# Attention scores for two heads at a time in three PSUM banks, with the second passes over the keys on half of the rows for each head

## The chip, the cores and the metric

The kernel runs on one core of one Trainium2 chip. The metric is the device time of one execution in microseconds (us). Shown is the median of three runs; a further execution was taken with the hardware profiler.

## The reference

Two transformer-like blocks run one after the other on 512 tokens of width 1024, in f32. The first block normalizes and modulates the tokens, projects them, does windowed attention with a short convolution beside it, and then a mixture of 16 experts. The second block has a spatial gate, a convolution of 31 taps and a projection. The change lies in the attention of the first block:

```
def block(i):                        # one of 4 blocks of 128 queries
    qb = q[128 i : 128 i + 128]      # 16 heads of 64, 4 heads share one key head
    kb, vb = the keys and values of block i - 1, i, i + 1 (those that exist)
    s_lat = qb . kb / 8              # masked to a distance of at most 128
    s_ctx = qb . k_ctx / 8           # 256 context keys
    p = softmax(concat(s_lat, s_ctx, sink of the head))
    return p_lat . vb + p_ctx . v_ctx
```

The result has to agree with f32 arithmetic, so most matmuls are made of several passes in f32r: an operand x is split into a rounded part hi and a remainder lo, and products of the parts are summed.

## The kernel before, in words

**Stages.** The context manager `tile_two_blocks` writes out the program engine by engine in a fixed order (`manual_schedule`): each engine runs its instructions in the order of the code, and waits on semaphores for its operands and for buffers. First comes the modulation, the norm and the sums for keys and values (up to line 661, about 74 us). Then the attention stage follows (lines 663 to 947), which runs the query projections (`q_group`), the projections of the short convolution (`ct_chunk` with `conv_posts`) and the attention itself, interleaved. Behind it lie the merge, the router, the experts, whose weights stream from HBM, and the second block.

**PSUM.** PSUM has eight banks of 512 f32 a partition. The pool `psA` (line 97) has six single banks with the tag `b`, which all matmuls of the stage take in turn (`bank`, line 100), and one buffer of two banks, `bank2` (line 103), for scores; before the stage that buffer holds sums for keys and values (`kvc`).

**Queries and keys.** For a group of four heads that share a key head, `q_group` computes the queries, `rope` turns them, and `qst` (line 702) holds for each head 128 columns: 64 of hi (written by ScalarE, line 703) and 64 of lo (by VectorE, line 704, two steps later). `q_T` (line 684) transposes these by TensorE, so that `qTs[g]` holds for each head hi on partitions 0 to 63 and lo on 64 to 127. `kT[g]` (line 627) holds two matrices over 768 keys (512 tokens, 256 context): `z = 0` has the keys' hi on both halves of the partitions, `z = 1` their lo on both halves. A matmul of all 128 rows therefore gives (q_hi + q_lo) . k_hi or (q_hi + q_lo) . k_lo.

**One block.** `Block` (line 819) is one of 16 pieces: key head g, query block b. A block at an end of the sequence (b = 0 or 3) sees 256 latent keys, one in the middle 384, and each 256 context keys. `scores(i)` (line 837) does one head: two passes over the latent keys (L846), two over the context keys (L849), all with 128 rows, into the buffer of two banks; one VectorE instruction (L852) adds the mask, takes the maximum and writes P to SBUF; a small one (L855) scales the maximum; ScalarE takes the exponential (L856). `normalize` (L861 to L866) divides by the sum on VectorE. `turn` transposes 128 columns of P of four heads (L872, L874), `value` multiplies with V (L881), two heads on two halves of the array's columns (`tile_position=(0, 64*h)`).

**Order.** The loop at the end (line 926) goes over the blocks; for each it makes five rounds, and in each of the first four it emits the scores of one head. Twice in each round `F.share()` emits a share of the projection steps, each of three matmuls (L297, L298, L299). `normalize` follows the scores of the last head, and in the rounds 0, 2 and 4 the block before is turned and multiplied with V:

```
for i in range(5):
    if new and i < 4:
        new.scores(i)
    F.share()
    if new and i == 3:
        new.normalize()
    if not i and older:
        older.late()
    if old:
        old.values(i)
    F.share()
```

`F.defer` puts a piece of work off by some steps. The weights of the next projection are split by ScalarE (L258) and VectorE (L256) while the one before runs; their loads are issued by SyncE (L218) when a buffer is free. Far behind, L1872 is a matmul on 64 rows between matmuls on 128 rows.

Of the kernel before, what the change touches and what calls it, by code (L numbers as in the profile page):

```python
# [9 lines left out]
F32 = mybir.dt.float32  # L10
F32R = mybir.dt.float32r
BF16 = mybir.dt.bfloat16
AF = mybir.ActivationFunctionType
OP = mybir.AluOpType
PSUM = bass.MemoryType.PSUM
# [3 lines left out]
NT = T // 128  # L19
# [44 lines left out]
def tile_two_blocks(ctx: ExitStack, tc: tile.TileContext, a, out):  # L64
    nc = tc.nc
    ACT, DVE, PE, POOL, SP = nc.scalar, nc.vector, nc.tensor, nc.gpsimd, nc.sync
# [27 lines left out]
    pe_ = ExitStack()  # L94
    ep = pe_.enter_context(tc.tile_pool(name="ep", bufs=6))
    pa = ExitStack()
    psA = pa.enter_context(tc.tile_pool(name="psA", bufs=6, space=PSUM))
    cur = {"ps": psA}

    def bank(name="pb", shape=(512,), dt=F32):  # L100
        return cur["ps"].tile([128] + list(shape), dt, name=name, tag="b")
# [1 line left out]
    def bank2(name="s2"):  # L103
        return cur["ps"].tile([128, 1024], F32, name=name, tag="s2", bufs=1)
# [6 lines left out]
    def C(name):  # L111
        s = CL[name]
        return cst[:, s] if s.stop <= nc0 else cst2[:, s.start - nc0:s.stop - nc0]

    ident = C("ident")
# [16 lines left out]
    for gi, g in enumerate(groups):  # L132
        r = 0
# [238 lines left out]
    F = Filler()  # L372


    p_ = bank()
# [156 lines left out]
    m0 = mod_rows(mws[0], ep)  # L532
# [26 lines left out]
    m0 = mod_rows(mws[1], ep)  # L559
# [22 lines left out]
    m0 = mod_rows(mws[2], ep)  # L582
# [11 lines left out]
    m0 = mod_rows(mws[3], ep)  # L594
# [12 lines left out]
    sp = pa.enter_context(tc.tile_pool(name="spA", bufs=2, reuse_waits="tile"))  # L607

    def rope(ps, t0):

        r = sp.tile([128, 2, 4, 64], F32, name="rope", tag="rope", bufs=1)
        s = sp.tile([128, 2, 4, 64], F32, name="ropes", tag="ropes", bufs=1)
        pv = ps.rearrange("p t (h d) -> p t h d", d=64)
        cs = C("cos").rearrange("p (t d) -> p t d", d=64)[:, t0:t0 + 2, None, :].to_broadcast([128, 2, 4, 64])
        DVE.tensor_mul(r, pv, cs)
        sn = C("sin").rearrange("p (t h z f) -> p t h z f", h=2, z=2, f=16)
        p5 = ps.rearrange("p t (q h z f) -> p t q h z f", h=2, z=2, f=16)
        s5 = s.rearrange("p t q (h z f) -> p t q h z f", h=2, z=2, f=16)
        for j in range(2):
            for h in range(2):  # L620
                DVE.tensor_mul(s5[:, j, :, h], p5[:, j, :, h, ::-1, :],
                               sn[:, t0 + j, None, h].to_broadcast([128, 4, 2, 16]))
        DVE.tensor_add(r, r, s)
        return r


    kT = [kv.tile([128, 2, 768], F32R, name=f"kT{g}", tag=f"kT{g}") for g in range(4)]
# [12 lines left out]
    def k_T(part, kst):  # L640
        for g in range(4):
            p_ = bank("pT", (2, 2, 128), F32R)
            for j in range(2):
                for z in range(2):
                    PE.transpose(p_[:, z, j, :], kst[:, j, g, z].rearrange("p a d -> p (a d)"), identr)
            dst = kT[g][:, :, part * 256:part * 256 + 256].rearrange("p z (j q) -> p z j q", j=2)
            ACT.activation(dst, p_.bitcast(F32), AF.Copy)
# [15 lines left out]
    sink8 = cp.tile([128, 16], F32, name="sink8")  # L663
# [4 lines left out]
    qTs = {}  # L668
# [9 lines left out]
    def q_group(g):  # L678
        i, w = nextw()
        nxt = W.steps(i + 1)  # L680
        qT = big("qT", [4, 512], F32R)
        qTs[g] = qT

        def q_T(tp, qst):
            for hp in range(2):
                p_ = bank("pT", (2, 2, 128), F32R)
                for hh in range(2):
                    for j in range(2):
                        PE.transpose(p_[:, hh, j, :], qst[:, j, 2 * hp + hh].rearrange("p a d -> p (a d)"), identr)
                dst = qT[:, 2 * hp:2 * hp + 2, tp * 256:tp * 256 + 256].rearrange("p i (j q) -> p i j q", j=2)  # L690
                ACT.activation(dst, p_.bitcast(F32), AF.Copy)
            if tp:
                qdone[0] = g

        for tp in range(2):
            pq = bank("pq", (2, 256))
            for j in range(2):
                for s, _ in enumerate(gemm_tc(pq[:, j], w, 2 * tp + j, hx)):
                    ahead(nxt, 8 * tp + 4 * j + s)
                    yield  # L700
            qr = rope(pq, 2 * tp)
            qst = sp.tile([128, 2, 4, 2, 64], F32R, name="qst", tag="qst", bufs=1)
            ACT.activation(qst[:, :, :, 0, :], qr, AF.Copy)
            F.defer(2, lambda qst=qst, qr=qr: DVE.tensor_sub(qst[:, :, :, 1, :], qr, qst[:, :, :, 0, :].bitcast(F32)))
            F.defer(9, lambda tp=tp, qst=qst: q_T(tp, qst))

    def ct_chunk(xs, post, hooks=None):
# [111 lines left out]
    class Block:  # L819


        def __init__(self, g, b):
            self.g, self.b = g, b
            self.kb = kb = [t for t in (b - 1, b, b + 1) if 0 <= t < NT]
            self.nl = nl = len(kb) * 128
            self.n = n = nl + 256

            if b == NT - 1:
                self.lo, self.co, self.s0, self.mask = 256, 0, 0, C("mask")[:, 0:512]
                self.keys = [4, 5] + kb  # L830
            else:
                self.lo, self.co, self.s0 = 512 - nl, 512, 512 - nl
                self.mask = C("mask")[:, 896 - n:]
                self.keys = kb + [4, 5]
            self.P, self.pt, self.nk = [], {}, n // 128

        def scores(self, i):
            g, kb, nl, n, lo, co = self.g, self.kb, self.nl, self.n, self.lo, self.co
            if not i:
                self.m4 = sp.tile([128, 4], F32, name="m4", tag="m4")  # L840
                self.sm = sp.tile([128, 4], F32, name="sm", tag="sm")
            m4, sm = self.m4, self.sm
            s2 = bank2()
            q = qTs[g][:, i, self.b * 128:self.b * 128 + 128]
            for z in range(2):
                PE.matmul(s2[:, lo:lo + nl], q, kT[g][:, z, kb[0] * 128:kb[0] * 128 + nl], start=(z == 0),  # L846
                          stop=(z == 1))
            for z in range(2):
                PE.matmul(s2[:, co:co + 256], q, kT[g][:, z, 512:768], start=(z == 0), stop=(z == 1))  # L849
            p_ = sp.tile([128, 640], F32, name="P", tag="P", bufs=8)  # L850
            self.P.append(p_)
            DVE.tensor_tensor_reduce(p_[:, :n], s2[:, self.s0:self.s0 + n], self.mask, 1.0,  # L852
                                     sink8[:, 4 * g + i:4 * g + i + 1], op0=OP.add, op1=OP.max,
                                     accum_out=m4[:, i:i + 1])
            DVE.tensor_scalar(m4[:, i:i + 1], m4[:, i:i + 1], -0.125, None, op0=OP.mult)  # L855
            ACT.activation(p_[:, :n], p_[:, :n], AF.Exp, bias=m4[:, i:i + 1], scale=0.125, accum_out=sm[:, i:i + 1])  # L856

        def normalize(self):
            g, sm = self.g, self.sm
# [8 lines left out]
        def turn(self, kk):  # L868

            p_ = bank("pT", (4, 128))  # L870
            for i in range(4):
                PE.transpose(p_[:, i, :], self.P[i][:, kk * 128:kk * 128 + 128], ident)  # L872
            self.pt[kk] = sp.tile([128, 2, 2, 128], F32, name="PT", tag="PT", bufs=4)
            ACT.activation(self.pt[kk], p_.rearrange("p (i h) q -> p i h q", h=2), AF.Copy)  # L874

# [26 lines left out]
    def order():  # L902
        n = 0
        for g in range(4):
            if g < 3:
                yield q_group(g + 1)
            for post in conv_posts(g):
                hooks = {}
                if n < 8:
                    if n % 2 == 0:  # L910
                        macc = sp.tile([128, 512], F32, name="macc", tag="macc", bufs=1)
                    hooks = mod_hooks(n % 2, macc, False, lambda c=24 + 2 * (n - 1), m=macc: mod_columns(c, m))
                yield ct_chunk(hx, post, hooks)
                n += 1

    todo = list(order())
    F.defer(6, lambda: k_T(0, kst[0]))
    F.defer(13, lambda: k_T(1, kst[1]))
    F.defer(20, lambda: k_T(2, kst[2]))
# [6 lines left out]
    for n, new in enumerate(blocks):  # L926
        if new:
            while qdone[0] < new.g:
                F.fill(1)
        for i in range(5):  # L930
            if new and i < 4:
                new.scores(i)
            F.share()
            if new and i == 3:
                new.normalize()
# [5 lines that stand above are left out]
        older, old = old, new  # L941
# [331 lines left out]
    x_, y_, d = l0, l1, 32  # L1273
    while d:
# [3 lines left out]
        x_, y_, d = y_, x_, d // 2  # L1278
# [19 lines left out]
    for t in range(NT):  # L1298
        PE.matmul(cnt[:, :, 16:32], ones, ge[:, t, None, 0:16].to_broadcast([128, NT, 16]), start=False,
                  stop=(t == NT - 1))  # L1300
# [152 lines left out]
    for p in range(8):  # L1453
# [21 lines left out]
        for n in range(2):  # L1475
            p_ = bank("pg", (4, 128))
# [231 lines left out]
    cin, co = {}, {}  # L1708
# [302 lines left out]
```

## Time and profile before

| what | value |
|---|---|
| median of 3 runs | 1662.72 us (1662.14 to 1664.51) |
| the profiled execution | 1664.67 us |
| its span, from the first to the last instruction | 1662.9 us |
| TensorE busy | 1613.8 us, 97% of the span |
| VectorE busy | 923.6 us, 56% |
| ScalarE busy | 565.7 us, 34% |
| mean granted TensorE clock | 0.997 |
| read from HBM | 333.62 MB |

The engines are called PE (TensorE matmul), PEld (TensorE weight load, which overlaps PE), DVE (VectorE), ACT (ScalarE), POOL (GpSimd) and SP (SyncE). L846 is line 846 of the kernel. Matmuls are pipelined, and the end of one is modelled, so a row can be longer than the distance to the next start. f32 matmuls that are not of the type f32r show as two records each. In a timeline, "x8" merges eight instructions of one line, and "[0.53 <-DVE m L852]" means that the engine stood idle for 0.53 us just before, until that instruction of VectorE ended.

### The profile page before, as it was taken

How to read it: one execution, taken by the hardware profiler on the slowest of the kernel's cores; microseconds unless marked ns; L12 is line 12 of the kernel's file. 1: busy time of each engine (PE TensorE's matmuls, PEld its weight loads, DVE VectorE, ACT ScalarE, POOL GpSimd, SP SyncE). 2: the span in 40 equal slices, each digit the busy share in tenths (PEclk: the TensorE clock that was granted, in tenths of full speed). 3: DMA queues.
4: the chain of work that ended last, by engine and by line, in shares of the span. 5: the costliest groups of instructions: out<-in, count | busy, mean ns of one | idle time of the engine just before them, and what ended most of it. 6: DMA issues, size and time to landing. Idle time of an engine off the chain costs nothing.

```text
span 1662.9 us, 20664 instructions
## 1 busy us (share of the span) xinstructions
PE 1613.8 (97%) x8266; PEld 1143.4 (69%) x8266; DVE 923.6 (56%) x1761; ACT 565.7 (34%) x1069; POOL 60.6 (4%) x74
## 2 busy tenths in 40 slices
PE   8999999999999999999999888999999999999998
PEld 5987878777888884333333333368898888877886
DVE  4667677665554342222132212178989999855555
ACT  4454545455223232000000000063335542354234
POOL 2000000000000000000000000010100001000000
PEclk9999999999999999999999999999999999999999
DMA  9223232212654599999999999943322323422341
GB/s 366 68 77 102 88 96 76 98 51 76 207 197 129 223 365 357 419 427 426 427 426 427 426 427 426 416 147 94 94 85 77 101 78 100 113 92 100 102 152 51
DMA packets 139412, 341.26 MB, mean 205 GB/s; under 512 B 6735, under 2 KB 91508, under 8 KB 115636
## 3 DMA queue, kind: packets, MB, share of 16 engines
q1 hardware_dynamic: 135504, 328.50, 52.6%
q0 software_dynamic: 2864, 8.67, 1.4%
q10 hardware_dynamic: 948, 2.76, 0.4%
q8 instruction: 65, 1.06, 0.3%
q14 instruction: 31, 0.25, 0.0%
HBM read 333.62 MB, written 6.29 MB: 204 GB/s over the span
## 4 chain that ended last, share of the span: by engine, by line
PE 43%; DMA 13%; DVE 2%; issue 1%; ACT 1%; POOL 0%; POOLq 0%; ACTq 0%; SPq 0%; DVEq 0%
PE pb L297 9%; PE pb L298 9%; PE pb L299 9%; DMA ew<-w_exp_up 5%; DMA ew<-w_exp_gate 5%; PE py L1382 3%; DMA ew<-w_exp_down 2%; PE pu L1382 2%; DMA xe<-x_d,ix 1%; PE pv L297 1%; PE pv L299 1%; PE pv L298 1%; PE pa__6391 L1382 1%; PE pa__6149 L1382 1%; PE pa__5907 L1382 1%
## 5 line engine op out<-in xcount | busy, mean ns | idle before, releaser
L256 DVE TENSOR_TENSOR wl<-wr,wh 128x512 fp32r<-128x512 f32 x340 | 230.5, 698 | 120.7 <-ACT wh L258 120.7
L258 ACT ACTIVATE wh<-wr 128x512 fp32r<-128x512 f32 x340 | 195.2, 621 | 111.2 <-PE pb L298 58.3
L1722 DVE SCALAR_TENSOR_TENSOR co<-cin,cols,co 128x512 f32<-128x512 f32 x240 | 190.2, 793 | 4.2
L297 PE MATMUL pb<-h2h,wh 128*128 128x512 f32 x432 | 170.7, 395 | 0.0
L299 PE MATMUL pb<-h2h,wl 128*128 128x512 f32 x432 | 168.3, 390 | 0.0
L298 PE MATMUL pb<-h2l,wh 128*128 128x512 f32 x432 | 168.3, 390 | 0.0
L297 PE MATMUL pb<-hxh,wh 128*128 128x512 f32 x320 | 129.2, 404 | 0.0
L1382 PE MATMUL pu<-ew,xe 128*64 128x512 f32 x512 | 115.9, 595 | 10.0 <-DMA ew<-w_exp_up 10.0
L298 PE MATMUL pb<-hxl,wh 128*128 128x512 f32 x320 | 125.2, 391 | 0.0
L299 PE MATMUL pb<-hxh,wl 128*128 128x512 f32 x320 | 125.0, 391 | 0.0
L1382 PE MATMUL py<-ew,hb 128*64 128x512 f32 x440 | 102.4, 596 | 3.3 <-DMA ew<-w_exp_down 3.3
L297 PEld LDWEIGHTS pb<-h2h,wh 128*128 128x128 f32 x432 | 81.1, 188 | 19.0 <-issue 2.4
L1382 PEld LDWEIGHTS pu<-ew,xe 128*64 128x64 f32 x512 | 38.5, 137 | 80.3 <-issue 61.9
L299 PEld LDWEIGHTS pb<-h2h,wl 128*128 128x128 f32 x432 | 81.1, 188 | 17.1
L298 PEld LDWEIGHTS pb<-h2l,wh 128*128 128x128 f32 x432 | 81.1, 188 | 16.8 <-issue 0.5
L856 ACT ACTIVATE P<-P,m 128x512 f32<-128x512 f32 (+1 forms) x64 | 49.8, 778 | 98.6 <-DVE m L855 96.3
L1399 DVE TENSOR_TENSOR xr<-pg,xr 128x512 f32<-128x512 f32 x64 | 41.5, 686 | 69.4 <-PE pg L1398 68.1
L1473 DVE TENSOR_TENSOR hb<-pu,hb 128x512 f32<-128x512 f32 x16 | 10.3, 685 | 122.1 <-PE pu L1382 77.1
L1382 PEld LDWEIGHTS py<-ew,hb 128*64 128x64 f32 x440 | 32.7, 137 | 61.7 <-issue 52.8
L852 DVE CUSTOM_DVE_ANT_0 P<-s,cst,sink 128x512 f32<-128x512 f32 (+1 forms) x64 | 52.1, 814 | 38.2 <-PE s L849 37.8
L299 PEld LDWEIGHTS pb<-hxh,wl 128*128 128x128 f32 x320 | 60.1, 188 | 13.3
L297 PEld LDWEIGHTS pb<-hxh,wh 128*128 128x128 f32 x320 | 60.2, 188 | 10.9 <-issue 1.9
(479 smaller groups left out, 2990.6 us busy)
## 6 DMA issues: line engine op xcount, KB each, us to landing
ew<-w_exp_gate SPq DMA_DIRECT2D x64, 1024.0 KB, 19.4
ew<-w_exp_up SPq DMA_DIRECT2D x64, 1024.0 KB, 19.5
wr<-w_in SPq DMA_DIRECT2D x58, 1024.0 KB, 5.8
ew<-w_exp_down SPq DMA_DIRECT2D x55, 1024.0 KB, 20.7
wr<-w_mod SPq DMA_DIRECT2D x16, 1024.0 KB, 5.2
wm<-w_mod SPq DMA_DIRECT2D x8, 1024.0 KB, 12.0
wr<-w_out SPq DMA_DIRECT2D x8, 1024.0 KB, 5.1
ew<-w_exp_down SPq DMA_DIRECT2D x16, 512.0 KB, 10.5
```

What stands on the lines that cost most here:

```text
L256: (lo_engine or DVE).tensor_tensor(lo[:, ks], raw[:, ks], hi[:, ks].bitcast(F32), op=OP.subtract)
L258: ACT.activation(hi[:, ks], raw[:, ks], AF.Copy)
L297: PE.matmul(ps, ah, bh, start=first, stop=False)
L298: PE.matmul(ps, ah, bl, start=False, stop=False)
L299: PE.matmul(ps, al, bh, start=False, stop=last)
L852: DVE.tensor_tensor_reduce(p_[:, :n], s2[:, self.s0:self.s0 + n], self.mask, 1.0, sink8[:, 4 * g + i:4 * g + i + 1], op0=OP.add, op1=OP.ma ...
L856: ACT.activation(p_[:, :n], p_[:, :n], AF.Exp, bias=m4[:, i:i + 1], scale=0.125, accum_out=sm[:, i:i + 1])
L1382: PE.matmul(ps[64 * e:64 * e + 64, n], lhs(k, e), tiles[e][kk][:, n * 512:n * 512 + 512], start=(k == 0), stop=(k == KT - 1), tile_positio ...
L1399: DVE.tensor_add(xrow(t, half(n)), p_, xrow(t, half(n)))
L1473: DVE.tensor_mul(hb[:, 0, n * 512:n * 512 + 512], pu[:, n], hb[:, 0, n * 512:n * 512 + 512])
L1722: DVE.scalar_tensor_tensor(co[ct], cin[ct][:, k:k + 512], ctap(k, ct), co[ct], op0=OP.mult, op1=OP.add)
```

## The change

Three things are changed together. Scores are made for two heads at a time (`scores(u)`, u = 0 or 1, in the rounds 0 and 2) into a buffer `s3` of three banks; for that the PSUM pool is closed before the stage and a new one opened with five single banks beside it. For odd heads the parts of the query are swapped, so that hi lies on partitions 64 to 127. The second pass over a group of keys (z = 1) uses the hi part of the query alone, 64 rows, with `tile_position=(64*i, 0)`: even heads on the upper half of the array's rows, odd heads on the lower. That leaves out q_lo . k_lo there. Where the two heads' scores for a group lie in one bank (the context keys of a middle block), both passes keep 128 rows. The mask and the order of the columns follow the new places.

```
-    psA = pa.enter_context(tc.tile_pool(name="psA", bufs=6, space=PSUM))
-    cur = {"ps": psA}
+    pz = ExitStack()
+    cur = {"ps": pz.enter_context(tc.tile_pool(name="psA", bufs=6, space=PSUM, reuse_waits="tile"))}
...
             qst = sp.tile([128, 2, 4, 2, 64], F32R, name="qst", tag="qst", bufs=1)
-            ACT.activation(qst[:, :, :, 0, :], qr, AF.Copy)
-            F.defer(2, lambda qst=qst, qr=qr: DVE.tensor_sub(qst[:, :, :, 1, :], qr, qst[:, :, :, 0, :].bitcast(F32)))
+            q4 = qst.rearrange("p j (u i) a d -> p (j u) (i a) d", i=2)
+            q2 = qr.rearrange("p j (u i) d -> p (j u) i d", i=2)
+            ACT.activation(q4[:, :, 0::3], q2, AF.Copy)
+            F.defer(2, lambda q4=q4, q2=q2: DVE.tensor_sub(q4[:, :, 1:3], q2, q4[:, :, 0::3].bitcast(F32)))
...
+            self.full = len(kb) == 3
+            if self.full:
+                self.cols = [(128, 512, 128, 256), (1024, 768, 768, 0)]
+            elif not b:
+                self.cols = [(0, 256, 0, 384), (1024, 1280, 1024, 384)]
             else:
-                self.lo, self.co, self.s0 = 512 - nl, 512, 512 - nl
-                self.mask = C("mask")[:, 896 - n:]
-                self.keys = kb + [4, 5]
+                self.cols = [(256, 0, 0, 0), (1280, 1024, 1024, 0)]
+            self.keys = [4, 5] + kb if b == NT - 1 else kb + [4, 5]
...
-            s2 = bank2()
-            q = qTs[g][:, i, self.b * 128:self.b * 128 + 128]
-            for z in range(2):
-                PE.matmul(s2[:, lo:lo + nl], q, kT[g][:, z, kb[0] * 128:kb[0] * 128 + nl], start=(z == 0),
-                          stop=(z == 1))
-            for z in range(2):
-                PE.matmul(s2[:, co:co + 256], q, kT[g][:, z, 512:768], start=(z == 0), stop=(z == 1))
...
+            s3 = cur["ps"].tile([128, 1536], F32, name="s3", tag="s3", bufs=1)
+            ks = (slice(kb[0] * 128, kb[0] * 128 + nl), slice(512, 768))
+
+            def product(i, c, z):
+                q = qTs[g][:, 2 * u + i, self.b * 128:self.b * 128 + 128]
+                c0, k_ = self.cols[i][c], ks[c]
+                d_ = s3[:, c0:c0 + k_.stop - k_.start]
+                if z and tiled:
+                    r = slice(64 * i, 64 * i + 64)
+                    PE.matmul(d_, q[r], kT[g][r, 1, k_], start=False, stop=True, tile_position=(64 * i, 0))
+                else:
+                    PE.matmul(d_, q, kT[g][:, z, k_], start=(z == 0), stop=(z == 1))
+
+            for c in range(2):
+
+                tiled = not c or not self.full
+                for i, z in ((0, 0), (1, 0), (0, 1), (1, 1)) if tiled else ((0, 0), (0, 1), (1, 0), (1, 1)):
+                    product(i, c, z)
+            for i in range(2):
+                h = 2 * u + i
+                s0, m0 = self.cols[i][2:]
...
+                DVE.tensor_tensor_reduce(p_[:, :n], s3[:, s0:s0 + n], C("mask")[:, m0:m0 + n], 1.0,
+                                         sink8[:, 4 * g + h:4 * g + h + 1], op0=OP.add, op1=OP.max,
+                                         accum_out=m4[:, h:h + 1])
...
-                PE.transpose(p_[:, i, :], self.P[i][:, kk * 128:kk * 128 + 128], ident)
+                c = (kk + 2) % 5 if self.full and i % 2 else kk
+                PE.transpose(p_[:, i, :], self.P[i][:, c * 128:c * 128 + 128], ident)
...
     todo = list(order())
+    pz.close()
+    cur["ps"] = pa.enter_context(tc.tile_pool(name="psQ", bufs=5, space=PSUM, reuse_waits="tile"))
...
-            if new and i < 4:
-                new.scores(i)
+            if new and i in (0, 2):
+                new.scores(i // 2)
```

## Rows read from the trace of the kernel before

**Rows 1.** The page, part 1: busy us, share of the span and instructions.
```profile
PE 1613.8 (97%) x8266; PEld 1143.4 (69%) x8266; DVE 923.6 (56%) x1761; ACT 565.7 (34%) x1069; POOL 60.6 (4%) x74
```

**Rows 2.** By stretch: length, busy PE, PEld, DVE, ACT, POOL, clock, DMA share, GB/s.
```profile
97.00:190.00 93.00, 88.97 (x573) 72.24 (x572) 67.39 (x173) 47.09 (x103) 0.00 (x0) 1.00 0.28 91
190.00:283.00 93.00, 91.33 (x582) 73.06 (x582) 66.42 (x165) 49.13 (x108) 0.00 (x0) 1.00 0.28 91
283.00:384.00 101.00, 101.00 (x579) 77.01 (x578) 62.29 (x153) 48.38 (x108) 0.00 (x0) 1.00 0.21 69
384.00:560.00 176.00, 176.00 (x765) 143.22 (x764) 93.78 (x141) 58.99 (x107) 0.00 (x0) 1.00 0.46 153
...
700.00:1060.00 360.00, 339.90 (x1524) 135.26 (x1520) 84.79 (x174) 29.07 (x44) 5.65 (x6) 1.00 1.01 426
```

**Rows 3.** Instructions of line 846: duration min/median/max in ns, first and last start, forms.
```profile
L846 PE MATMUL s<-kT,qT x128: 274/333/445, 97.5 to 364.5; 128*128 128x256 f32 x64, 128*128 128x384 f32 x64
```

**Rows 4.** Waits of TensorE, 97 to 384 us: total, times, longest in us.
```profile
PE s L846 <- DVE m L852: 5.2, 8, 1.6
PE pT L872 <- DVE P L866: 0.2, 1, 0.2
```

**Rows 5.** Timeline of TensorE, scores of one head: start us, length us.
```profile
258.60 0.51 PE L846 MATMUL s<-kT,qT 128*128 128x384 f32 x2
258.95 0.40 PE L849 MATMUL s<-kT,qT 128*128 128x256 f32 x2
259.19 0.28 PE L297 MATMUL pq<-wh,hxh 128*128 128x256 f32 x1
```

**Rows 6.** Timeline of TensorE around a matmul on 64 rows.
```profile
1475.47 0.39 PE L298 MATMUL pb<-h2l,wh 128*128 128x512 f32 x1
1475.70 0.39 PE L299 MATMUL pb<-h2h,wl 128*128 128x512 f32 x1
1476.02 0.50 PE L1872 MATMUL pr<-rvs,strip 64*128 64x512 f32 x1
1476.44 0.50 PE L297 MATMUL pb<-h2h,wh 128*128 128x512 f32 x1
1476.79 0.40 PE L298 MATMUL pb<-h2l,wh 128*128 128x512 f32 x1
```

**Rows 7.** Timeline of the weight loads at the same place.
```profile
1475.47 0.19 PEld L299 LDWEIGHTS pb<-h2h,wl 128*128 128x128 f32 x1
1476.02 0.18 PEld L1872 LDWEIGHTS pr<-rvs,strip 64*128 64x128 f32 x1 [0.35 <-issue]
```

**Rows 8.** Timeline of TensorE: value matmuls on half columns, then transposes.
```profile
225.87 1.08 PE L881 MATMUL po<-PT,V 128*64 128x256 f32 x8
226.88 1.09 PE L872 MATMUL pT<-cst,P 128*128 128x128 f32 x8
227.73 0.48 PE L297 MATMUL pb<-hxh,wh 128*128 128x512 f32 x1
```

**Rows 9.** Timeline of TensorE between two heads, with a wait.
```profile
234.26 0.41 PE L849 MATMUL s<-kT,qT 128*128 128x256 f32 x2
...
237.96 0.40 PE L299 MATMUL pb<-hxh,wl 128*128 128x512 f32 x1
238.88 0.50 PE L846 MATMUL s<-kT,qT 128*128 128x256 f32 x2 [0.53 <-DVE m L852]
```

**Rows 10.** Timeline of VectorE in the same stretch.
```profile
234.24 1.68 DVE L866 TENSOR_SCALAR P<-P,sm 128x512 f32<-128x512 f32 x4
...
238.07 0.74 DVE L852 CUSTOM_DVE_ANT_0 P<-s,cst,sink 128x512 f32<-128x512 f32 x1
```

**Rows 11.** Timeline of all engines at the start of the stage.
```profile
74.07 0.28 PE L297 MATMUL pq<-wh,hxh 128*128 128x256 f32 x1
74.08 0.87 DVE L621 TENSOR_TENSOR ropes<-ka,cst 128x128 f32<-128x128 f32 x4
...
77.57 1.08 ACT L660 ACTIVATE V<-va 128x512 f32<-128x512 f32 x2
```

More of the change, by code (lines that the diff above doesn't have):

```diff
@@ L826, in __init__, with scores @@
             self.n = n = nl + 256
-            if b == NT - 1:
-                self.lo, self.co, self.s0, self.mask = 256, 0, 0, C("mask")[:, 0:512]
-                self.keys = [4, 5] + kb
-            else:
-                self.lo, self.co, self.s0 = 512 - nl, 512, 512 - nl
-                self.mask = C("mask")[:, 896 - n:]
-                self.keys = kb + [4, 5]
+            self.full = len(kb) == 3
[3 more added lines that the diff above has]
+                self.cols = [(0, 256, 0, 384), (1024, 1280, 1024, 384)]
+            else:
+                self.cols = [(256, 0, 0, 0), (1280, 1024, 1024, 0)]
+            self.keys = [4, 5] + kb if b == NT - 1 else kb + [4, 5]
             self.P, self.pt, self.nk = [], {}, n // 128
-        def scores(self, i):
-            g, kb, nl, n, lo, co = self.g, self.kb, self.nl, self.n, self.lo, self.co
-            if not i:
+        def scores(self, u):
+            g, kb, nl, n = self.g, self.kb, self.nl, self.n
+            if not u:
                 self.m4 = sp.tile([128, 4], F32, name="m4", tag="m4")
@@ L842, in scores @@
             m4, sm = self.m4, self.sm
-            s2 = bank2()
-            q = qTs[g][:, i, self.b * 128:self.b * 128 + 128]
-            for z in range(2):
-                PE.matmul(s2[:, lo:lo + nl], q, kT[g][:, z, kb[0] * 128:kb[0] * 128 + nl], start=(z == 0),
-                          stop=(z == 1))
-            for z in range(2):
-                PE.matmul(s2[:, co:co + 256], q, kT[g][:, z, 512:768], start=(z == 0), stop=(z == 1))
-            p_ = sp.tile([128, 640], F32, name="P", tag="P", bufs=8)
@@ L851, in scores @@
[L851 to L856, printed above, removed]
+            s3 = cur["ps"].tile([128, 1536], F32, name="s3", tag="s3", bufs=1)
@@ new lines, in scores @@
+            for c in range(2):
[5 more added lines that the diff above has]
+                s0, m0 = self.cols[i][2:]
+                p_ = sp.tile([128, 640], F32, name="P", tag="P", bufs=8)
+                self.P.append(p_)
+                DVE.tensor_tensor_reduce(p_[:, :n], s3[:, s0:s0 + n], C("mask")[:, m0:m0 + n], 1.0,
+                                         sink8[:, 4 * g + h:4 * g + h + 1], op0=OP.add, op1=OP.max,
+                                         accum_out=m4[:, h:h + 1])
+                DVE.tensor_scalar(m4[:, h:h + 1], m4[:, h:h + 1], -0.125, None, op0=OP.mult)
+                ACT.activation(p_[:, :n], p_[:, :n], AF.Exp, bias=m4[:, h:h + 1], scale=0.125,
+                               accum_out=sm[:, h:h + 1])
```

## The prediction

> **What bounds the kernel now.** I read the page first: TensorE is busy 97% of the span, VectorE 56% [rows 1]. The change lies in the attention stage, so I cut the span into stretches next: from 97 to 384 us the score matmuls run among the projection matmuls, and there TensorE is busy 88.97 of 93, 91.33 of 93 and 101.00 of 101 us, at a granted clock of 1.00 (the level of 2.4 GHz), while VectorE has about 30% to spare [rows 2]. So the stage takes what its stream of matmuls takes, plus 5.7 us in which TensorE stands. The waits of TensorE in that stretch name the cause of nearly all of it: 8 score matmuls wait, 5.2 us together, until VectorE has read the scores of the head before (L852) out of the one score buffer [rows 4]. What counts is therefore how much of TensorE's stream the change cuts or adds, and which of these waits it ends. Behind the stage TensorE is full up to 560 us (176.00 of 176), and from 700 to 1060 us the DMA engines are (share 1.01, on expert weights) [rows 2]. Those loads go into buffers that the work ahead sets free, in program order, so I pass a shift of the stage on to the end one for one.
>
> **What a score pass costs.** Matmuls are pipelined, so I count from start to start. Two 384-column passes of a full block start at 258.60, the next line at 258.95: 0.175 us each. The two 256-column passes take from 258.95 to 259.19: 0.12 each [rows 5]. Each pass loads its weights behind the matmul before it, so loads cost nothing here.
>
> **What is cut.** For each pair of heads the second passes over a column group run on 64 rows for each head, on different halves of the array and into different PSUM banks. If the two run side by side, one pass time goes per such group. Half of the L846 passes have 256 columns and half 384 [rows 3]: 8 blocks at the ends of the sequence (two column groups of 256) and 8 in the middle. A middle block tiles only its own keys (384), since its context columns share a bank. With 2 pairs a block that is 16 groups of 384 and 32 of 256: 16 x 0.175 + 32 x 0.12 = 2.8 + 3.8 = **6.6 us saved**. That they do run side by side is seen nowhere before for half rows. The nearest row is for half columns: eight value matmuls (two records each of 128x64 weights, 256 columns) take from 225.87 to 226.88, 0.126 each, though the transposes behind them need (227.73 - 226.88) / 8 = 0.106 for 128 columns of the same f32, which makes 0.21 for 256 [rows 8]. Such halves overlap, and I take it for rows too; the bounds are one pass saved and none.
>
> **What is added: going to half rows and back.** The same program has one matmul on 64 rows in the midst of full ones, L1872, eight times. Full ones start every 0.23 us (1475.47, 1475.70). Then L1872 starts 0.32 after its predecessor, the next full one 0.42 after that, and the one behind it 0.35 later: 1.09 us from 1475.70 to 1476.79 for three matmuls of 0.23 [rows 6]. The surplus is 0.40 us: 0.09 before the switch in, 0.09 before the switch back, and twice about 0.11 in which the new weights are loaded in the open: L1872's load starts with its matmul, at 1476.02, where the load of an ordinary one starts a whole matmul earlier (1475.47 for 1475.70) [rows 6, 7]. Every tiled group of the change lies between full matmuls: a middle pair switches in and back once, an end pair twice (its context group begins with full passes again). That is 16 + 32 = 48 groups x 0.40 = **19.2 us added**, three times what they save. Net: +12.6 us. The bounds for one group are 0.18 (the switches alone) and 0.40; I take 0.40, because L1872 has the same 64 rows, 128 weight columns and type.
>
> The Trainium skill, page TensorEngine Tiling (Array Packing), section Key Properties, says that changing the tiling mode drains the engine, and that different tiles can load weights and multiply in parallel. The 0.09 agrees with the first half; were the second half to hold for the first load of a group and for the load on the way back, a group would cost the 0.18 and the sum would be that of rival B2 below.
>
> **What ends: the waits of TensorE.** Example: head 0's last score matmul starts at 234.26; VectorE is still scaling the old block's P (234.24) and reads the scores only at 238.07 for 0.74 us; TensorE is ready at 237.96 + 0.23 = 238.19 and starts head 1 at 238.88 [rows 9, 10]. The row says 0.53 idle, but the loss from start to start is 0.69, since the modelled end of the matmul before lies 0.16 later; and the second pass is 0.11 late as well (the two take 0.50 instead of 0.39 or so). So the 8 waits cost 5.2 + 8 x (0.16 + 0.11) = 7.4 us. Afterwards a buffer is asked for once per pair. A block has 287 / 16 = 17.9 us and ten shares of projection work; four shares, some 7.2 us, lie between the pairs of a block and six before the next block. The reading that ended 4.3 us after its matmuls would end some 1.0 us later (a second head to read), at 5.3, still inside. I take **all 7.4 us as regained**; the bounds are 0 and 7.4. What would be late next is the turning of P (L872), which waits on VectorE's scaling; that scaling stays at its place in the program, with the last two heads' scores out earlier.
>
> **Edits at or near nothing.** The copies of the query parts (L703, L704) move as many elements with another stride, on engines with time to spare. The mask is a slice, the order of the odd heads' columns an index. Two reads and two exponentials now come together, so a weight split behind them on VectorE or ScalarE is up to a head's work later; the next weights are prepared one chunk ahead, and if that cover went, a projection matmul would wait about 1 us at a time. One bank less for everything else: TensorE waits on no bank now [rows 4], so 0, up to 2 us. No DMA is added or moved, and SyncE's queue only follows the buffers. The new pool takes over banks that the key and value sums held: query matmuls start at 74.07, the rope reads one of those banks in four instructions from 74.08 that take 0.87, and the copies of V begin at 77.57 for 1.08 [rows 11]. The first query bank costs nothing, 0.9 or up to 4.6 us, depending on which it is; I take **0.9**.
>
> **Sum.** 19.2 - 6.6 - 7.4 + 0.9 = +6.1 us. The profiled execution took 1664.67 us (span 1662.9), so it would become 1670.8. The median of the three runs is 1662.72; on that footing it is **1668.8 us**. The waits of another run may differ by a microsecond. I call 0.2%, 3.3 us, about what a measurement of this kernel can tell from no change.
>
> **Rivals.**
> B1: one of the two open loads hides, the other not: a group costs 0.29, the sum is 13.9 - 6.6 - 7.4 + 0.9 = +0.8, 1663.5 us. For it: loads hide everywhere else. Against: at L1872 neither hides [rows 6, 7].
> B2, the other side: both hide and only the switches are left, 48 x 0.18 = 8.6, sum -4.5, 1658.2 us. This decides from a group price of (6.6 + 7.4 - 0.9) / 48 = 0.27 us down. For it: two tiles of half the array could be loaded while the other half works. Against: the matmul before a group always fills all rows, as at L1872.
> C: the two half-row passes do not run side by side (or load one after the other). Then nothing is saved: +12.7, 1675.4 us. Against: the value matmuls [rows 8]; but those are halves by column.
> D: the waits move elsewhere instead of ending, because VectorE is behind in the first hundred microseconds of the stage: +13.5, 1676.2 us. Against: after 283 us TensorE has no idle time at all [rows 2].
>
> **Chances.** Forecast 0.52 (of which 0.39 beyond +3.3 us and 0.13 within), B1 0.13, B2 0.16, C 0.12, D 0.07. Slower: 0.39 + 0.12 + 0.07 = 0.58. Same: 0.26. Faster: 0.16. The range runs from B2's time to C's, 1658.0 to 1675.5: it leaves out D and the outer tails of B2 and C, under 0.2 together.
>
> **What the next profile would show.** Right: half-row matmuls in pairs a few ns apart; the first load of each group starting with its matmul; surplus of about 0.40 us around a group; no idle time of score matmuls on L852; a stage some 5 us longer, and all behind it shifted by as much. Wrong: a surplus under 0.27 us; pairs that start a whole pass apart; TensorE waiting on P or on a bank.

## The result, and the profile after

The median after is 1672.34 us (1670.19 to 1673.65, five runs), against 1662.72 us before (five runs by now). The ratio is 1.0053 with a 95% interval of 1.0041 to 1.0064: the changed kernel is slower by 8.8 us, between 6.8 and 10.6 (the two medians lie 9.6 us apart). Forecast was 6.1 us slower. The profiled execution took 1673.65 us. Its page, in the lines that answer to [rows 1] and the span:

```profile
span 1671.9 us, 20707 instructions
...
PE 1626.9 (97%) x8266; PEld 1141.8 (68%) x8266; DVE 922.6 (55%) x1761; ACT 566.7 (34%) x1069; POOL 60.7 (4%) x74
```

The span is 9.0 us longer, and TensorE is busy for longer, with as many instructions. To see where the stage ends, take the first matmul behind it, on the split attention output `osh`, in the view of that tile (duration, first and last start). Before:

```profile
L297 PE MATMUL pb<-osh,wh x64: 392/394/793, 395.3 to 540.8; 128*128 128x512 f32 x64
```

After:

```profile
L297 PE MATMUL pb<-osh,wh x64: 392/394/793, 403.9 to 549.5; 128*128 128x512 f32 x64
```

So 8.6 of the 9.0 us are there at the end of the attention stage, and the last of these matmuls, 145 us on, is still 8.7 us late: the rest of the program is shifted, hardly changed. The waits of TensorE in the stage after the change (total, times, longest), to set against [rows 4]:

```profile
PE pT L689 <- ACT PT L898: 2.8, 2, 2.4
PE pq L297 <- DVE ropes L621: 0.9, 1, 0.9
```

Every wait for the score buffer is gone. There are two new ones: 0.9 us at the first query bank, and 2.8 us in which the transposes of the queries (L689) wait until ScalarE has copied a transposed P (L898).

A pair of heads of a middle block on TensorE (timeline: start, length):

```profile
257.67 0.51 PE L862 MATMUL s<-kT,qT 128*128 128x384 f32 x2
258.11 0.44 PE L860 MATMUL s<-kT,qT 64*128 64x384 f32 x2
258.48 0.73 PE L862 MATMUL s<-kT,qT 128*128 128x256 f32 x4
259.05 0.28 PE L297 MATMUL pq<-wh,hxh 128*128 128x256 f32 x1
```

The same moments in the weight loads:

```profile
258.11 0.19 PEld L860 LDWEIGHTS s<-kT,qT 64*128 64x128 f32 x2 [0.25 <-issue]
258.48 0.53 PEld L862 LDWEIGHTS s<-kT,qT 128*128 128x128 f32 x4 [0.18 <-issue]
```

And a pair of an end block on TensorE:

```profile
228.26 0.40 PE L862 MATMUL s<-kT,qT 128*128 128x256 f32 x2
228.58 0.38 PE L860 MATMUL s<-kT,qT 64*128 64x256 f32 x2
228.90 0.50 PE L862 MATMUL s<-kT,qT 128*128 128x256 f32 x2
229.32 0.39 PE L860 MATMUL s<-kT,qT 64*128 64x256 f32 x2
229.64 0.50 PE L297 MATMUL pb<-hxh,wh 128*128 128x512 f32 x1
229.98 0.39 PE L298 MATMUL pb<-hxl,wh 128*128 128x512 f32 x1
```

Both half-row passes of a group start together (two matmuls in 0.44 us, of which one is as long; in all 48 groups of the trace the second starts 3 to 4 ns after the first), so they do run side by side. But their loads start with them, and so does the load of the full pass behind them. The middle pair takes 259.05 - 257.67 = 1.38 us, where four passes of 0.175 and four of 0.12 took 1.18 [rows 5]: 0.20 more. The end pair takes 229.98 - 228.26 = 1.72, less the 0.23 of the L297 behind it, which starts the next one late: 1.49, against 8 x 0.12 = 0.96: 0.53 more. Over 16 pairs of each kind that is 3.2 + 8.5 = 11.7 us. The pairs shown are typical: the medians over all 16 of a kind are 1.39 us for a middle pair and 1.49 for an end pair, against 1.18 and 0.96 in the run with full rows below, which makes 12.0 us.

### The profile page after: what moved, and what is told of

Read it like the earlier page. It is cut to its first block, busy times and chain, and to the rows that moved or that the text cites. A ratio compares the mean times of both kernels' runs of the same rounds, so it can differ in the third digit from the quotient of the medians.

```text
span 1671.9 us, 20707 instructions
## 1 busy us (share of the span) xinstructions
PE 1626.9 (97%) x8266; PEld 1141.8 (68%) x8266; DVE 922.6 (55%) x1761; ACT 566.7 (34%) x1069; POOL 60.7 (4%) x74
## 4 chain that ended last, share of the span: by engine, by line
PE 40%; DMA 16%; DVE 2%; issue 1%; ACT 1%; POOL 0%; POOLq 0%; SPq 0%; ACTq 0%; DVEq 0%
PE pb L297 9%; PE pb L298 9%; PE pb L299 9%; DMA ew<-w_exp_gate 6%; DMA ew<-w_exp_up 5%; DMA ew<-w_exp_down 5%; PE py L1408 3%; PE pu L1408 2%; PE pv L297 1%; PE pv L299 1%; PE pv L298 1%; PE pa__5879 L1408 1%; PE pa__6121 L1408 1%; PE py L1555 1%; PE pb L1669 1%
## 5 line engine op out<-in xcount | busy, mean ns | idle before, releaser
L297 PE MATMUL pb<-h2h,wh 128*128 128x512 f32 x432 | 170.7, 395 | 0.0
L297 PE MATMUL pb<-hxh,wh 128*128 128x512 f32 x320 | 131.0, 409 | 0.0
L297 PEld LDWEIGHTS pb<-h2h,wh 128*128 128x128 f32 x432 | 81.1, 188 | 19.0 <-issue 2.4
L299 PEld LDWEIGHTS pb<-h2h,wl 128*128 128x128 f32 x432 | 81.1, 188 | 17.1
L1499 DVE TENSOR_TENSOR hb<-pu,hb 128x512 f32<-128x512 f32 x16 | 10.3, 686 | 122.5 <-PE pu L1408 77.5
L297 PEld LDWEIGHTS pb<-hxh,wh 128*128 128x128 f32 x320 | 60.3, 188 | 13.5 <-issue 1.9
```

What stands on the lines that cost most here:

```text
L297: PE.matmul(ps, ah, bh, start=first, stop=False)
L299: PE.matmul(ps, al, bh, start=False, stop=last)
```

## The experiments

Each run has a short name, e1 to e8. Differences to the kernel before are worked out from each ratio and 1663 us.

**All passes on full rows (e1).** One line, everything else as changed:

```
-                tiled = not c or not self.full
+                tiled = False
```

> Scores of two heads at a time in three banks as in the changed kernel, but all second passes on 128 rows, so that no matmul of the stage switches to half rows. Theory (the half rows cost 0.40 us a group, 48 groups, and save 6.6 us, and the ten us of the change come from there): 12.6 us less than the changed kernel's 1672.3, so 1659.7 us, which is some 3 us less than before, because the waits for the score buffer (7.4 us) stay ended. Rival (the pairing of heads or the smaller pool makes the loss, half rows are neutral): 1668 us or more.

Measured: ratio 0.9993 (0.9984 to 1.0002), 1.2 us below before, so 10.0 us below the changed kernel. The half rows carry the loss; pairing heads and the smaller pool, taken together, do not. The size is 2.6 us short of the theory, and the gain against before is 1.2 us and not 3. The pair itself is as it should be (timeline of TensorE):

```profile
255.25 1.33 PE L862 MATMUL s<-kT,qT 128*128 128x384 f32 x8
256.43 0.28 PE L297 MATMUL pq<-wh,hxh 128*128 128x256 f32 x1
```

1.18 us for eight passes. What differs is in the waits of TensorE in the stage:

```profile
PE pT L689 <- ACT PT L898: 3.2, 3, 2.4
PE pq L297 <- DVE ropes L621: 0.9, 1, 0.9
PE pb L792 <- ACT oT L908: 0.5, 1, 0.5
PE pT L896 <- DVE P L889: 0.5, 1, 0.5
```

That is 5.1 us, where the changed kernel has 3.7. A TensorE that comes sooner waits longer for the others: 11.7 - 1.4 = 10.3 us is about what the runs show. In the two profiled executions the stage itself, from the first query matmul (74.9 us changed, 72.8 here) to the first on `osh` (403.9 and 390.9), is 10.9 us shorter here, of which 1.7 is the low clock described in the last section.

**Half rows in middle blocks only (e2).** 16 groups in place of 48:

```
-                tiled = not c or not self.full
+                tiled = not c and self.full
```

> Half rows only in the middle blocks, 16 groups of 384 columns instead of 48 groups. Theory (a price of 0.40 us for each group, whatever its columns, and 0.12 us saved by a group of 256): 32 x 0.28 = 9.0 us less than the changed kernel, 1663.3 us. Rival (the price grows with the columns of a group, as it would if half-row passes streamed more slowly): the 16 groups of 384 would carry 43% of the cost, and the time would be about 1665.2 us; rival (half rows are neutral): 1672 us.

Measured: ratio 1.0014 (1.0005 to 1.0023), 2.3 us above before, 6.5 below the changed kernel. This total lies nearer to the rival by columns (7.1) than to the theory (9.0), but with the intervals of both kernels, some 1.5 and 1.9 us to either side, it settles nothing; and e2 has 4.5 us of waits in the stage where the changed kernel has 3.7. Against e1 the 16 groups cost 3.5 us, 0.22 each, which is about the 0.20 read above. The rows of the changed kernel settle the rival: a group of 384 columns costs 0.20 + 0.175 = 0.38, one of 256 columns 0.53 / 2 + 0.12 = 0.39. The price is one for each group.

**Each half-row pass alone (e3).** The order of the passes:

```
-                for i, z in ((0, 0), (1, 0), (0, 1), (1, 1)) if tiled else ((0, 0), (0, 1), (1, 0), (1, 1)):
+                for i, z in ((0, 0), (0, 1), (1, 0), (1, 1)):
```

> The half-row second passes of the two heads no longer follow each other: the order in each group is first and second pass of the one head, then of the other. That makes 96 groups of one half-row matmul instead of 48 of two. Theory (each group costs 0.40 us, and the two of a pair run side by side in the changed kernel): 48 x 0.40 = 19.2 us more, and the 6.6 us of the overlap are lost too, so 1698.1 us. Rival (half-row passes did not run side by side in the changed kernel either): 1691.5 us. Rival (a group costs only the two drains, 0.18 us): 1672.3 + 8.6 + 6.6 = 1687.5 us.

Measured: 1696.36 us, ratio 1.0193 (1.0177 to 1.0208), 32.1 us above before, 23.3 above the changed kernel. Theory had 25.8, the rivals 19.2 and 15.2. A middle pair in its timeline of TensorE:

```profile
271.35 0.34 PE L862 MATMUL s<-kT,qT 128*128 128x384 f32 x1
271.62 0.44 PE L860 MATMUL s<-kT,qT 64*128 64x384 f32 x1
271.99 0.44 PE L862 MATMUL s<-kT,qT 128*128 128x384 f32 x1
272.36 0.44 PE L860 MATMUL s<-kT,qT 64*128 64x384 f32 x1
272.72 0.74 PE L862 MATMUL s<-kT,qT 128*128 128x256 f32 x4
273.30 0.28 PE L297 MATMUL pq<-wh,hxh 128*128 128x256 f32 x1
```

1.95 us, 0.57 more than the 1.38 of the changed kernel: a pass of 0.175 that no longer overlaps, and a second group at 0.39. Both rivals fall. The missing 2.5 us are again partly in waits: those for ScalarE are 1.4 us here instead of 2.8.

**Both second passes on the same half (e6).** The query parts of odd heads stay in place, and

```
-                    r = slice(64 * i, 64 * i + 64)
-                    PE.matmul(d_, q[r], kT[g][r, 1, k_], start=False, stop=True, tile_position=(64 * i, 0))
+                    r = slice(0, 64)
+                    PE.matmul(d_, q[r], kT[g][r, 1, k_], start=False, stop=True, tile_position=(0, 0))
```

> The changed kernel with the query parts of odd heads not swapped, so that both second passes of a group use rows 0 to 63, one after the other, with the same 48 groups. Theory (in the changed kernel the two run side by side on two halves): 16 x 0.175 + 32 x 0.12 = 6.6 us more than the changed kernel, up to 1 us of it taken from waits, so 14.4 to 15.4 us above the kernel before. Rival (they already ran one after the other): the same as the changed kernel, 8.8 us above.

Measured: 1678.04 us, ratio 1.0093 (1.0078 to 1.0109), 15.5 us above before, 6.7 above the changed kernel: what the overlap had been worth. The timeline of a middle pair:

```profile
257.42 0.51 PE L862 MATMUL s<-kT,qT 128*128 128x384 f32 x2
257.86 0.61 PE L860 MATMUL s<-kT,qT 64*128 64x384 f32 x2
258.40 0.74 PE L862 MATMUL s<-kT,qT 128*128 128x256 f32 x4
```

From the half-row passes to the next line it is 0.54 us, against 258.48 - 258.11 = 0.37 in the changed kernel.

**The pools alone (e4).** The kernel before, one head at a time in two banks, with the pool closed ahead of the stage and opened again with five banks:

```
-    psA = pa.enter_context(tc.tile_pool(name="psA", bufs=6, space=PSUM))
-    cur = {"ps": psA}
+    pz = ExitStack()
+    cur = {"ps": pz.enter_context(tc.tile_pool(name="psA", bufs=6, space=PSUM, reuse_waits="tile"))}
...
     todo = list(order())
+    pz.close()
+    cur["ps"] = pa.enter_context(tc.tile_pool(name="psQ", bufs=5, space=PSUM, reuse_waits="tile"))
```

> The kernel before with the change of pools alone: the pool is closed ahead of the stage and opened again with five single banks instead of six, scores still one head at a time. Theory (the first query bank waits 0.9 us for the rope, and with five banks TensorE waits some 2 to 3 us for ScalarE to empty a transposed P early in the stage): 1662.7 + 0.9 + 2 to 3, so 1665.6 to 1666.6 us. Rival (five banks are enough, the wait came from the two exponentials that now stand together on ScalarE): 1663.6 us.

Measured: ratio 1.0008 (0.9999 to 1.0017), 1.3 us above before, which is less than the theory's 2.9 to 3.9 and nearer to the rival's 0.9; the interval holds the rival and not the theory. The waits of TensorE show why:

```profile
PE s L846 <- DVE m L852: 3.8, 7, 1.6
PE pT L689 <- ACT PT L874: 1.4, 1, 1.4
PE pq L297 <- DVE ropes L621: 0.9, 1, 0.9
```

Both stories hold in part. With five banks the query transposes wait for ScalarE even with single heads, 1.4 us; but 1.4 us of the waits for scores go in exchange (3.8 instead of 5.2). In the changed kernel the same wait is 2.4 us long, 1.0 more, which is one exponential: in e4 ScalarE makes one exponential and starts the copy of the transposed P 0.82 us after it (116.64 and 117.46), in the changed kernel it makes two and starts the copy 1.81 us after the first (116.36 and 118.17). ScalarE in the changed kernel:

```profile
116.36 0.83 ACT L878 ACTIVATE P<-P,m 128x640 f32<-128x640 f32 x1 [4.07 <-DVE m L877]
117.09 0.19 ACT L878 ACTIVATION_READ_ACCUMULATOR P<-P,m 128x1 f32 x1
117.34 0.83 ACT L878 ACTIVATE P<-P,m 128x640 f32<-128x640 f32 x1
118.08 0.19 ACT L878 ACTIVATION_READ_ACCUMULATOR P<-P,m 128x1 f32 x1
118.17 1.06 ACT L898 ACTIVATE PT<-pT 128x512 f32<-128x512 f32 x2
```

ScalarE stands idle for 4.07 us for the maximum of the first head, with the copies that would free banks queued behind two exponentials. VectorE in that time works on other things in its order:

```profile
112.21 1.68 DVE L889 TENSOR_SCALAR P<-P,sm 128x512 f32<-128x512 f32 x4
113.80 1.53 DVE L772 SCALAR_TENSOR_TENSOR macc<-wr,sT,macc 128x512 f32<-128x512 f32 x2
115.25 0.88 DVE L874 CUSTOM_DVE_ANT_0 P<-s,cst,sink 128x640 f32<-128x640 f32 x1
```

**Full rows, exponentials later (e5).** From that reading, two edits on top of e1: `scores` collects the exponentials and the loop issues them behind the old block's transposes, and the pool is closed after the first query group:

```
...
-            if new and i in (0, 2):
-                new.scores(i // 2)
+            exps = new.scores(i // 2) if new and i in (0, 2) else []
...
             if old:
                 old.values(i)
+            for f in exps:
+                f()
             F.share()
```

> All second passes on 128 rows as in e1, and two edits against the waits that e1 still had: the exponentials of a pair are issued behind the copies of the old block's transposed P on ScalarE, and the pool is closed one projection group later, when the rope has read its bank. Theory (TensorE's 2.4 us wait near 116 us comes from copies queued on ScalarE behind exponentials that wait for VectorE, while no bank is free; the first 0.9 us from the rope): those waits, 4.1 us in e1, go, and the time is about 5 us below the kernel before. Rival (exponentials issued later make the scaling of P late, and TensorE waits on P instead): no more than 1 us below, as e1.

Measured: 1658.25 us, ratio 0.9971 (0.9960 to 0.9981), 4.8 us below before. This version beats both kernels, by as much as the theory gave. The two edits were not run apart; what each gives is read from the waits alone. Its waits of TensorE in the stage:

```profile
PE pb L297 <- DVE yT L818: 0.8, 1, 0.8
PE pT L689 <- DVE ropes L621: 0.7, 1, 0.7
PE pT L898 <- DVE P L891: 0.4, 1, 0.4
```

Of 3.2 us for ScalarE nothing is left. The rope's 0.9 has become 0.7 at a later bank. One group of transposes waits for P, but that is no sign of the rival: the kernel before has the same wait at the same group (timeline of TensorE, before):

```profile
113.38 1.95 PE L872 MATMUL pT<-cst,P 128*128 128x128 f32 x8 [0.25 <-DVE P L866]
```

**Half rows, exponentials later (e8).** The changed kernel with the same two edits:

> The changed kernel, half rows and all, with the two edits of e5 against the waits. It stands against e5 for the price of the half rows alone, with hardly a wait in either. Theory (48 groups at 0.40 us, 6.6 us saved): 12.6 us more than e5, about 7.6 us above the kernel before. Rival (the changed kernel against e1 showed the full price): 10 us more than e5.

Measured: 1668.39 us, ratio 1.0034 (1.0021 to 1.0048), 5.7 us above before and 10.5 above e5. The number is nearer to the rival's 10 than to the theory's 12.6. Of that, 11.7 is what the pair rows give. e5 has lost the rest to its wait on P, which e8 has not; the transposes there (timeline of TensorE, e5):

```profile
112.59 1.96 PE L898 MATMUL pT<-cst,P 128*128 128x128 f32 x8 [0.43 <-DVE P L891]
114.30 0.48 PE L297 MATMUL pb<-hxh,wh 128*128 128x512 f32 x1
```

They start 0.43 us late and take 114.30 - 112.59 = 1.71 instead of the 0.85 of [rows 8], 1.3 us in all. The stage itself, counted as in e1, takes 315.0 us in the profiled execution of e5 and 325.8 in that of e8, at a granted clock of 1.00 in both: 10.8 us for the half rows.

## Why the prediction was right, and where its sizes were off

The direction, the range and the mechanism held. Term by term:

- **The price of going to half rows and back** was taken from one matmul, L1872, as 0.40 us a group, and measured 0.38 to 0.39 in the changed kernel's pairs, the same for 256 and 384 columns (e3's second groups cost as much; e2's total does not decide). The overlap was worth what was forecast: 6.6 us, 6.7 in e6. Net, 11.7 (12.0 by the medians) instead of 12.6 us.
- **The waits for scores**: all were to end, and none is left. What that gave back was put at 7.4 us. Counted from start to start in the trace before, the 8 score matmuls come 6.5 us late and their second passes 0.8: 7.3, as taken. The difference agrees: 0.9 + 11.7 + 2.8 and some 1.7 for a low clock (below) make 17.1; the stage is 8.6 longer, so about 8.5 came back. Most of the rest is the group of transposes at 113.38 us: in the kernel before it loses 1.3 us to late P, in the changed kernel 0.2.
- **The first query bank** cost 0.9 us, by the rope, as taken.
- **"One bank less for everything else: TensorE waits on no bank now, so 0, up to 2 us"** is the term that was wrong. That no bank is waited for with six says nothing of five. The profile shows 2.8 us, above the 2 it allowed (TensorE waiting on a bank was named as a sign of being wrong, and it came), and e4 that the pools alone make 1.4 of them; the other part is the sentence on the two exponentials, which looked at weight splits behind them and not at the copies that free banks. This term, with the clock that fell behind it, added 4.5 us that were not in the sum; the cheaper groups (0.9) and the other waits that ended (1.1) took 2.0 off. So the profiled execution lost 9.0 us and not 6.1, and that the sum came as near owes something to errors in both directions.
- **Passing the shift on one for one** held here: 8.6 at the end of the stage, 9.0 at the end. In single executions it holds within 2 us only: e1 is 4.4 us early at the end of the stage and 2.6 at the end, e6 11.1 and 13.1 us late, e5 6.3 and 7.7 early. The clock differs there too: from 900 to 1000 us it is 0.97 in e1 and e6, 1.00 before and in e5. And 2.2 of e1's 4.4 us arise ahead of the stage, which starts at 72.8 us, a wait of 0.9 included, against 74.1 before. So compare a stage from its start to its end.

Of the rivals, B1 and B2 (a load that hides) fall by the load rows, where each starts with its matmul, and by the price of 0.39 us against their 0.29 and 0.18. C (no overlap) falls by e6. D (the waits move instead of ending) was right on a small scale: not the score waits themselves, but 2.8 us on ScalarE behind the same late VectorE.

## What to carry to other kernels

A group of matmuls on part of the rows between full ones pays about 0.39 us here, with 256 columns as with 384, so it has to save more than that, and a pair of 256 or 384 columns (0.12 or 0.175 saved) is far too short. It seems to follow, though no run here tried it, that tiled passes belong together in long groups. A score buffer asked for half as often, with twice the time to empty it, ended its waits without a faster engine. On an engine that runs in order, as e5 against e1 suggests (4.8 us below before instead of 1.2, with two edits at once), put the copies that free a bank ahead of work that still waits for another engine.

## What the runs showed that was not expected

The 2.4 us wait of the query transposes was followed by a fall of TensorE's clock. Stretches of 2 us of the changed kernel (length, busy time by engine, then the granted clock, the third number from the end):

```profile
116.00:118.00 2.00, 0.39 (x5) 0.24 (x3) 1.88 (x9) 1.58 (x3) 0.00 (x0) 1.00 0.73 172
118.00:120.00 2.00, 1.20 (x7) 1.02 (x8) 0.21 (x1) 2.00 (x6) 0.00 (x0) 0.96 0.91 352
120.00:122.00 2.00, 2.00 (x6) 1.60 (x5) 0.71 (x2) 2.00 (x5) 0.00 (x0) 0.50 0.00 0
122.00:124.00 2.00, 2.00 (x8) 1.21 (x8) 0.46 (x1) 0.25 (x1) 0.00 (x0) 0.69 0.00 0
```

After two stretches with 0.39 and 1.20 us of work the clock is at 0.50, the level of 1.2 GHz, though TensorE is full again. The matmuls show it in the timeline:

```profile
120.01 0.63 PE L297 MATMUL pb<-hxh,wh 128*128 128x512 f32 x1
120.44 0.63 PE L298 MATMUL pb<-hxl,wh 128*128 128x512 f32 x1
```

They start 0.43 us apart instead of 0.23. The shares add up to 0.08 + 1.00 + 0.62 = 1.7 us lost. The profile of e1 has a wait of the same 2.4 us, and its clock stays at 1.00:

```profile
116.00:118.00 2.00, 1.29 (x8) 1.16 (x9) 0.30 (x1) 2.00 (x6) 0.00 (x0) 1.00 0.87 334
118.00:120.00 2.00, 2.00 (x12) 1.77 (x11) 0.71 (x2) 2.00 (x5) 0.00 (x0) 1.00 0.00 0
```

The profile of e2 has the wait of 2.4 us too, and its clock falls (0.80 and 0.50 in the stretches from 116 to 120 us); e6, with 2.1 us, stays at 1.00. So such a wait cost 1.7 us more than its length in two of four profiled executions and nothing in the other two. Nor does a fall need a wait: in e3 the clock is at 0.70, 0.50, 0.50 and 0.59 in the stretches of 2 us from 258 to 266 us, with TensorE busy for 2.00 us of each, which loses 3.4 us. What decides it stays open, and whether it makes the spread of the runs (1670.19 to 1673.65) was not tried.
